# Seven products earlier for one pair, and another cut of the stores of turned pages

## The chip, the cores and the metric

The kernel runs on one core of a Trainium2 chip. The metric is the device time of one execution in microseconds (us); of several runs the median is taken. A profile is one more execution, taken with the hardware profiler.

## What is computed

The reference is a two-layer encoder over 256 tokens with a model width of 4096, all in float32. Cut to what matters:

```python
for l in range(2):
    h = rmsnorm(x, norm_w[l])
    proj = h @ w_in[l]                       # 256 x 4096 @ 4096 x 11264
    aq, ak, av, ag, rq, rk, rv, rg = split(proj)
    # attention: 16 query heads on 4 key heads, norm and rotation of q and k
    a_out = silu(ag) * gqa_attention(rope(rmsnorm(aq)), rope(rmsnorm(ak)), av)
    # retention: 8 heads, forward and backward decays
    r_out = silu(rg) * rmsnorm(bidirectional_retention(rope(rq), rope(rk), rv))
    x = x + concat(a_out, r_out) @ w_out[l]  # 256 x 4096 @ 4096 x 4096
return rmsnorm(x, final_norm)
```

The two projections of each layer hold nearly all of the arithmetic.

## The kernel before

**Blocks, pairs, products.** A projection is cut into blocks of 1024 output columns: 11 for `w_in` and 4 for `w_out` in each layer, 30 blocks that the text numbers 0 to 29 by `plan.index` (layer 0: 0 to 10 and 11 to 14; layer 1: 15 to 25 and 26 to 29), or counts from 0 within its projection. The sum over 4096 runs over 16 pairs of 128-row slices. For one pair, a block is a product of a 2 x 2 by a 2 x 2 arrangement of 128 x 128 and 128 x 512 tiles. Such a product can be made with eight tile products, or with seven by taking sums of tiles first (Strassen and Winograd). Each tile product is three matmuls of 128 x 512, because float32 numbers are split into a high and a low part of a shorter format (hi x hi, lo x hi and hi x lo).

**Weight pages.** A pair of eight reads two pages of weights of 128 x 1024 in a block, named A and B. A pair of seven has four: A, B and the sums T and U. Each page goes through a raw buffer (`wraw`, loaded by DMA from SP's queue; sums in `wsum`, made on VectorE), a cast on ScalarE (`whi`) and a subtraction on VectorE (`wlo`). Some B pages are fetched and split through POOL's queue instead (`fhi`, `flo`).

**Operand forms.** `x` is kept in SBUF in the forms that the products need: `x8h`, `x8l` and a third form `x3` for pairs of eight, `x7h`, `x7l` with seven forms for pairs of seven. Four tables say which pair takes seven:

- `SEVEN`: pairs that take seven everywhere.
- `AFTER`: one dictionary for the input projection and one for the output projection; `{10: (3, 1)}` says that pair 10 takes seven from block 3 on in layer 0 and from block 1 on in layer 1. A pair that starts with eight is converted by `sevenfold` when its last product of the block before has been issued.
- `EXTRA`: pair 4, which is kept in the form of eight and converted with more room.
- `WIDE`: all pairs whose operand has room for seven forms. It is the same set before and after.

`DEFER` puts off the third form (`third`) of the pairs of layer 0 until block 2; blocks 0 and 1 of layer 0 use other eight products that don't need it.

**The order of work.** The order of the instructions on each engine is fixed when the program is built. TensorE's products follow the order of pages of each block (`ORDERS`, or `in_groups` where there is none). All other steps are placed around them by a planner, which keeps a model of the engines and of the DMA queues and picks, whenever VectorE or ScalarE is free in its model, the step with the earliest due time (`pump`). `SETS` changes the planner's settings in single blocks: `SOFT` is the due time of ordinary steps, `PE_REST` how long the inputs of a small attention product should have been ready before TensorE takes it up. Engines wait only on semaphores, each in its own order.

**Turned pages.** Attention and retention work with transposed pages. `turned` transposes blocks of 32 x 32 on VectorE within SBUF; `store` then writes the page (128 x 1024) to DRAM so that the rest of the transposition is done by the addresses, in four DMAs on POOL's queue; `fetch` or a later read brings it back, when all four have landed. The DRAM tiles are `p_dram`, `q_dram`, `g_dram`, `k_dram`, `rk_dram`, `rq_dram` and `next_dram`. Every instruction is recorded by a helper on line 463, so the profile names all of them L463; tiles tell them apart.

Of the kernel before, what the change touches and what calls it, by code (L numbers as in the profile page):

```python
# [19 lines left out]
SEQ = 256  # L20
# [13 lines left out]
BLK = 32  # L34
# [14 lines left out]
SOFT = 7.0  # L49
# [3 lines left out]
PE_REST = 3.0  # L53
# [12 lines left out]

SPLITS = 3

SEVEN = (0, 2, 5, 8, 11, 13)

MORE = ()

AFTER = ({10: (3, 1)}, {4: (1, 1), 10: (1, 1)})

EXTRA = (4,)

WIDE = tuple(sorted({*SEVEN, *MORE, *AFTER[0], *AFTER[1]} - {*EXTRA}))

# [8 lines left out]
FORMS = 2  # L87

ORDERS = {
# [21 lines left out]

SETS = {
    (0, 'PE_REST'): 2.0,
    (1, 'SLACK'): 2.0,
    (5, 'PE_REST'): 4.0,
    (6, 'PE_REST'): 4.0,
    (8, 'DUE'): 50.0,
# [102 lines left out]
def sevens_of(l, second, b):  # L220

    late = [_p for _p, _b in AFTER[second].items() if b >= _b[l]]
    return tuple(sorted({*SEVEN, *(MORE if second else ()), *late}))


def parsed(text):

    return [(int(_v[:-1]), "ATBU".index(_v[-1])) for _v in text.split()]


def in_groups(sevens, first=False):

    order = []
    for group in [tuple(range(_a, _b)) for _a, _b in zip(sevens, sevens[1:] + (NP,))]:
        one, rest = group[:1], group[1:]
        if first:
            order += [(_p, _k) for _p in NATIVE if _p in group for _k in (PAGE_A, PAGE_B)]
            one = [_p for _p in one if _p not in NATIVE]
            rest = [_p for _p in rest if _p not in NATIVE]
        one = [(_p, _k) for _p in one for _k in (PAGE_A, PAGE_T, PAGE_B, PAGE_U)]  # L240
        rest = [(_p, _k) for _p in rest for _k in (PAGE_A, PAGE_B)]
        for _v in one:
            order += [_v] + rest[:1]
            rest = rest[1:]
        order += rest
    return order


def slots_of(order, sevens, first=False, plain=False):

    for _p, _k in order:
        if _p in sevens and not (first and _p in NATIVE):
            yield [(_b, _p, (ALL, _a), _k, _h) for _b, _a, _pg, _h in SEVEN_PRODUCTS if _pg == _k]
        else:
            eight = PLAIN_PRODUCTS if plain else EIGHT_PRODUCTS
            yield [(_b, _p, (_i, _a), _k, _h) for _b, _i, _a, _pg, _h in eight if _pg == _k]
# [273 lines left out]
def hybrid_encoder(  # L530
# [14 lines left out]
    ve, ac, pe, gp, sy = (  # L545
        Engine(e, engine, model, active)
        for e, engine in (("V", nc.vector), ("A", nc.scalar), ("P", nc.tensor), ("G", nc.gpsimd), ("S", nc.sync))
    )
# [39 lines left out]
    def drop(n=1):  # L588

        def dropped():  # L590
            held[0] -= n
            own(-n)

        do(dropped)
# [12 lines left out]
    def plan_of(l, second, b):  # L607
# [11 lines left out]
        plan.sevens = sevens_of(l, second, plan.b)  # L619
        pages = parsed(ORDERS[plan.index]) if plan.index in ORDERS else in_groups(plan.sevens, plan.start)  # L620
        for slot in slots_of(pages, plan.sevens, plan.start, plan.plain):
# [404 lines left out]
    def split_pair(p, v, whole, stage):  # L1026
# [56 lines left out]
        else:  # L1083
            late = AFTER[stage % 2].get(p, (None,) * DEPTH)[stage // 2]
            if p in EIGHTS:
# [59 lines left out]
    def sevenfold(p, phase):  # L1145

        while held[0] + pledged() >= PAGES:
            yield
        hi, lo = operand[p][:2]
        v = page([P, 7, P], "xf")  # L1150
        if p in WIDE:
            ve.tensor_add(v[:, :4, :], f32(hi)[:, :4, :], f32(lo)[:, :4, :])
        else:
            both = [f32(w).rearrange("p k (m t) -> p m k t", m=MT) for w in (hi, lo)]
            ve.tensor_add(v[:, :4, :].rearrange("p (m k) t -> p m k t", m=MT), *both)
        yield from forms(v, v[:, 2, :], v[:, A22N, :])
        if p in WIDE:
            ac.copy(hi[:, 2:7, :], v[:, 2:7, :])
            yield
            ve.tensor_sub(lo[:, 2:7, :], v[:, 2:7, :], f32(hi)[:, 2:7, :])  # L1160
        else:
            room = operand[p][3].rearrange("p a b t -> p (a b) t")
            if phase not in spare:
                spare[phase] = t(sp, [P, 2 * MT, HD], "cs", dt=F32R)
            n = 2 * EXTRA.index(p)
            more = spare[phase][:, n : n + 2, :]
            halves = hi[:, :, P:], lo[:, :, P:]
            ac.copy(halves[0], v[:, 2:4, :])
            ac.copy(room[:, 0:3, :], v[:, 4:7, :])
            yield  # L1170
            ve.tensor_sub(halves[1], v[:, 2:4, :], f32(halves[0]))
            ve.tensor_sub(room[:, 3, :], v[:, 4, :], f32(room[:, 0, :]))
            ve.tensor_sub(more, v[:, 5:7, :], f32(room[:, 1:3, :]))
            pieces = [(hi[:, k, :P], lo[:, k, :P]) for k in range(2)] + [(hi[:, k, P:], lo[:, k, P:]) for k in range(2)]
            pieces += [(room[:, 0, :], room[:, 3, :])] + [(room[:, 1 + k, :], more[:, k, :]) for k in range(2)]
            do(partial(sevenths.__setitem__, p, pieces))
        drop()
        do(partial(changed.__setitem__, p, phase))
        yield
# [269 lines left out]

    def store(room, to):  # L1450

        to = to.rearrange("(b e) (a f) -> a e b f", e=BLK, a=4)
        for a in range(4):
            gp.dma_start(to[a], room[BLK * a : BLK * (a + 1), :].rearrange("e (b f) -> e b f", b=4))
        drop()

    def fetch(src, name):
# [48 lines left out]
    def rotary(v, L, kind, to):  # L1506
# [34 lines left out]
        drop()  # L1541
        yield
        store(v, to)
        return rs if kind == "aq" else None

# [15 lines left out]
    def attention_pair(g, h, kv, qT, rs, done):  # L1561
# [38 lines left out]
        drop()  # L1600
        yield
        store(room, p_dram[2 * (g % 2) + h // 2])
        yield

# [26 lines left out]
    def attention_group(L, g, gacc, qacc):  # L1631
        def gates():
            yield from gate(gacc, L)
            room = page([P, KG * SEQ], "room")
            turned(gacc, room)
            drop()
            yield
            store(room, g_dram[g % 2])

        yield from gates()  # L1640
        while "aq" not in L.tables:
            yield
        rs = yield from rotary(qacc, L, "aq", q_dram[g % 2])
        yield
        L.rs[g] = rs
# [218 lines left out]
    def block(plan, after_pair, combine, then):  # L1864
# [67 lines left out]
        def there(p):  # L1932
            if first_order and p in NATIVE:
                return p in as_it_comes
            if plan.b >= AFTER[second].get(p, (N_IN,) * DEPTH)[plan.layer] > 0 and changed.get(p) != plan.phase:
                return False
# [32 lines left out]
        def ended(n, name, p, k):  # L1969
# [6 lines left out]
            while over and all(not left[q] for q in range(min(over))):  # L1976
                q = min(over)
                over.remove(q)
                after_pair(q)
                if AFTER[second].get(q, (0,) * DEPTH)[plan.layer] == plan.b + 1:  # L1980
                    one = Lane(sevenfold(q, plan.phase))
# [374 lines left out]
```

## Time and profile before

| | |
|---|---|
| time, median of 3 runs | 2580.09 us (2575.61 to 2580.73) |
| the profiled execution's own time | 2579.86 us |
| its span, first to last instruction | 2578.1 us |
| TensorE (PE) busy | 2562.9 us, 11479 matmuls |
| VectorE (DVE) busy | 2365.2 us |
| ScalarE (ACT) busy | 1708.5 us |
| GpSimd (POOL) busy | 455.5 us |
| DMA | 685.95 MB, 266 GB/s on average |
| mean granted TensorE clock | 0.998 |

A row of a group of instructions names line, engine, operation, what it writes and reads, shapes and count, then busy time, mean time of one in ns, and the idle time before them with what ended it. PEld is TensorE's weight load, which overlaps the matmuls. A row of a wait names who waited for whom, the total in us, how often, and the longest. A row of a DMA gives the kilobytes of one and the median time from issue to landing.

### The profile page before, as it was taken

To read this page: it belongs to the slowest core of one execution; us is meant where nothing else is said; L and a number is where in the kernel's file an instruction comes from. 1 tells how busy PE (TensorE), PEld (TensorE's weight loads), DVE (VectorE), ACT (ScalarE), POOL (GpSimd) and SP (SyncE) were. 2 spreads that over 40 slices of the span, in tenths; PEclk is the share of its full clock that TensorE was granted. 3 is DMA by queue.
4 is the path that set the end of the run, shared out by engine and by line. 5 is a ranking of instruction groups with operands and counts; after the bars stand their busy time and mean duration, and the time that the engine had idled before them with its cause. 6 is when DMAs were issued, how large, how long until landed. Compare 5 with 4: busy or idle time off the path is not lost.

```text
span 2578.1 us, 34225 instructions
## 1 busy us (share of the span) xinstructions
PE 2562.9 (99%) x11479; PEld 2118.9 (82%) x11479; DVE 2365.2 (92%) x2882; ACT 1708.5 (66%) x2482; POOL 455.5 (18%) x672
## 2 busy tenths in 40 slices
PE   9999999999999999999999999999999999999998
PEld 6888888887888888888888888888888888888886
DVE  7999998999989899998999999999999799999887
ACT  7766676666655768665786666775676566776665
POOL 0112221211111111111221112212211111111111
PEclk9999999999999999999999999999999999999999
DMA  8988888888678787988998888888887787888986
GB/s 305 325 258 285 281 268 263 282 271 259 209 237 263 233 279 237 293 263 255 328 309 266 264 276 273 291 251 290 272 270 227 238 250 239 267 260 262 269 261 212
DMA packets 197680, 685.95 MB, mean 266 GB/s; under 512 B 24192, under 2 KB 24448, under 8 KB 197504
## 3 DMA queue, kind: packets, MB, share of 16 engines
q1 hardware_dynamic: 126880, 447.80, 48.9%
q0 software_dynamic: 70624, 235.97, 35.9%
q8 instruction: 90, 1.47, 0.2%
q14 instruction: 86, 0.70, 0.1%
HBM read 636.49 MB, written 47.19 MB: 265 GB/s over the span
## 4 chain that ended last, share of the span: by engine, by line
PE 95%; DMA 2%; DVE 1%; issue 1%; ACT 0%; POOL 0%; POOLq 0%; DVEq 0%; ACTq 0%
PE M L463 91%; PE ps L463 4%; DMA wraw<-in_w_in 1%; DVE wlo L463 1%; DMA pT<-p_dram 0%; DMA flo<-in_w_out 0%; DVE wsum L463 0%; DVE cb L463 0%; ACT whi L463 0%; POOL p_dram L463 0%; DVE ca L463 0%; POOL rs L463 0%; DVE pTl L463 0%; ACT full L463 0%; DVE room L463 0%
## 5 line engine op out<-in xcount | busy, mean ns | idle before, releaser
L463 ACT CAST whi<-wraw 128x1024 fp32r<-128x1024 f32 (+1 forms) x816 | 759.4, 935 | 353.5 <-PE M L463 283.3
L463 DVE TENSOR_TENSOR wlo<-wraw,whi 128x1024 fp32r<-128x1024 f32 (+1 forms) x816 | 868.2, 1075 | 54.0 <-ACT whi L463 50.0
L463 ACT CAST whi<-wsum 128x1024 fp32r<-128x1024 f32 x418 | 438.6, 1050 | 290.7 <-DVE wsum L463 140.5
L463 DVE TENSOR_TENSOR wlo<-wsum,whi 128x1024 fp32r<-128x1024 f32 x418 | 509.3, 1219 | 94.0 <-ACT whi L463 64.0
L463 PE MATMUL M<-whi,x7h 128*128 128x512 f32 x1465 | 571.0, 390 | 2.0 <-DVE ca L463 1.3
L463 PE MATMUL M<-whi,x7l 128*128 128x512 f32 x1465 | 570.4, 389 | 0.0
L463 PE MATMUL M<-wlo,x7h 128*128 128x512 f32 x1465 | 476.4, 389 | 0.1
L463 PE MATMUL M<-whi,x8h 128*128 128x512 f32 x1168 | 455.1, 390 | 0.0
L463 PE MATMUL M<-whi,x8l 128*128 128x512 f32 x1168 | 454.8, 389 | 0.2 <-DVE x8l L463 0.2
L463 PE MATMUL M<-wlo,x8h 128*128 128x512 f32 x1168 | 362.2, 389 | 0.0
L463 PEld LDWEIGHTS M<-whi,x7h 128*128 128x128 f32 x1465 | 275.1, 188 | 60.4 <-ACT whi L463 3.0
L463 PEld LDWEIGHTS M<-wlo,x7h 128*128 128x128 f32 x1465 | 274.7, 188 | 58.3 <-DVE wlo L463 1.2
L463 PEld LDWEIGHTS M<-whi,x7l 128*128 128x128 f32 x1465 | 275.1, 188 | 56.3 <-issue 0.2
L463 DVE TENSOR_TENSOR wsum<-wraw 128x1024 f32<-128x1024 f32 x209 | 254.5, 1218 | 4.2 <-DMA wraw<-in_w_out 2.3
L463 PEld LDWEIGHTS M<-whi,x8h 128*128 128x128 f32 x1168 | 219.3, 188 | 46.3 <-DVE ca L463 1.2
L463 PEld LDWEIGHTS M<-wlo,x8h 128*128 128x128 f32 x1168 | 219.2, 188 | 45.7
L463 PEld LDWEIGHTS M<-whi,x8l 128*128 128x128 f32 x1168 | 219.3, 188 | 45.6 <-DVE x8l L463 0.7
L463 PE MATMUL M<-whi,x 128*128 128x512 f32 x742 | 229.6, 389 | 0.0
L463 ACT ACTIVATE flo<-fhi 128x1024 fp32r<-128x1024 f32 (+1 forms) x140 | 147.0, 1050 | 121.4 <-PE M L463 120.5
L463 POOL DMA_DIRECT2D fhi<-in_w_in x102 | 56.6, 554 | 878.2 <-PE M L463 877.6
L463 PEld LDWEIGHTS M<-whi,x 128*128 128x128 f32 x742 | 138.8, 188 | 28.7
L463 PE MATMUL M<-fhi,x8l 128*128 128x512 f32 x414 | 161.1, 389 | 0.0
(275 smaller groups left out, 3179.7 us busy)
## 6 DMA issues: line engine op xcount, KB each, us to landing
wraw<-in_w_in SPq DMA_DIRECT2D x598, 512.0 KB, 5.8
wraw<-in_w_out SPq DMA_DIRECT2D x218, 512.0 KB, 6.0
fhi<-in_w_in POOLq DMA_DIRECT2D x102, 512.0 KB, 4.7
flo<-in_w_in POOLq DMA_DIRECT2D x102, 512.0 KB, 8.2
fhi<-in_w_out POOLq DMA_DIRECT2D x35, 512.0 KB, 5.6
flo<-in_w_out POOLq DMA_DIRECT2D x35, 512.0 KB, 8.0
full<-next_dram POOLq DMA_DIRECT2D x24, 512.0 KB, 8.4
p_dram<-room POOLq DMA_DIRECT2D x64, 128.0 KB, 5.2
```

Source lines behind the costliest of these rows:

```text
L463: op.call()
```

## The change

Three things are changed. Pair 10 takes seven products from block 1 on in layer 0's input projection (before: from block 3 on) and in all four blocks of its output projection (before: from block 1 on). Pair 2 leaves `SEVEN` and is listed in `AFTER` instead: seven everywhere as before, but in layer 0's output projection from block 2 on only. Page orders for blocks 1 and 3 are added, those for 11 and 19 replaced, and two settings are added, for blocks 0 and 2. And `store` cuts a page into four parts of 128 partitions by 256 columns instead of 32 partitions by 1024 columns.

```diff
-SEVEN = (0, 2, 5, 8, 11, 13)
+SEVEN = (0, 5, 8, 11, 13)
...
-AFTER = ({10: (3, 1)}, {4: (1, 1), 10: (1, 1)})
+AFTER = ({2: (0, 0), 10: (1, 1)}, {2: (2, 0), 4: (1, 1), 10: (0, 1)})
...
 ORDERS = {
+    1: '0A 0T 1A 1B 0B 0U 2A 3A 2T 3B 2B 4A 2U 4B 5A 6A 5T 5B 6B 7A 5U 7B 8A 9A 8T 9B 8B 8U 10A 10T 10B 10U 11A 12A 11T 12B 11B 11U 13A 14A 13T 14B 13B 13U 15A 15B',
+    3: '0A 0T 1A 1B 0B 0U 2A 3A 2T 3B 2B 4A 2U 4B 5A 6A 5T 6B 5B 7A 8A 5U 7B 9A 8T 9B 8B 8U 10A 10T 10B 10U 11A 12A 11T 12B 11B 11U 13A 14A 13T 14B 13B 13U 15A 15B',
...
-    11: '0A 0T 0B 1A 1B 0U 2A 3A 2T 3B 2B 4A 2U 4B 5A 6A 5T 6B 5B 7A 5U 7B 8A 9A 8T 9B 8B 10A 8U 10B 11A 12A 11T 12B 11B 11U 13A 14A 13T 14B 13B 13U 15A 15B',
-    19: '0A 0T 1A 1B 0B 0U 2A 3A 2T 3B 2B 4A 2U 4B 5A 6A 5T 6B 5B 7A 5U 7B 8A 9A 8T 9B 8B 8U 10A 12A 10T 10B 10U 11A 11T 12B 11B 11U 13A 14A 13T 14B 13B 13U 15A 15B',
+    11: '0A 0T 1A 1B 0B 2A 0U 2B 3A 3B 4A 4B 5A 6A 5T 6B 5B 7A 5U 7B 8A 9A 8T 10A 9B 8B 8U 10T 10B 10U 11A 12A 11T 12B 11B 11U 13A 14A 13T 14B 13B 13U 15A 15B',
+    19: '0A 0T 1A 1B 0B 0U 2A 3A 2T 3B 2B 4A 2U 4B 5A 6A 5T 6B 5B 7A 5U 7B 8A 9A 8T 9B 8B 8U 10A 12A 10T 10B 11A 11T 12B 10U 11B 11U 13A 14A 13T 14B 13B 13U 15A 15B',
...
 SETS = {
     (0, 'PE_REST'): 2.0,
+    (0, 'SOFT'): 3.0,
     (1, 'SLACK'): 2.0,
+    (2, 'PE_REST'): 4.0,
...
     def store(room, to):
-        to = to.rearrange("(b e) (a f) -> a e b f", e=BLK, a=4)
-        for a in range(4):
-            gp.dma_start(to[a], room[BLK * a : BLK * (a + 1), :].rearrange("e (b f) -> e b f", b=4))
+        to = to.rearrange("(b e) (a f) -> b a e f", e=BLK, a=4)
+        for b in range(4):
+            gp.dma_start(to[b], room[:, b * SEQ : (b + 1) * SEQ])
         drop()
```

## The prediction

> **What bounds the kernel now.** I read the page's busy times and its chain first, then the chain in order of time, then TensorE's waits, then stretches of one block each.
>
> ```profile
> span 2578.1 us, 34225 instructions
> PE 2562.9 (99%) x11479; PEld 2118.9 (82%) x11479; DVE 2365.2 (92%) x2882; ACT 1708.5 (66%) x2482; POOL 455.5 (18%) x672
> ...
> PE 95%; DMA 2%; DVE 1%; issue 1%; ACT 0%; POOL 0%; POOLq 0%; DVEq 0%; ACTq 0%
> ...
> L463 DVE TENSOR_TENSOR wsum<-wraw 128x1024 f32<-128x1024 f32 x209 | 254.5, 1218 | 4.2 <-DMA wraw<-in_w_out 2.3
> ```
>
> TensorE is busy in all but 15.2 us of the span, and it is 95% of the chain that ended last. The last row counts the seven-product pairs: one such sum for each, 209 in all. A busy TensorE can still be slowed, so the chain in order of time gives its pace:
>
> ```profile
> 598.17 9.73 DMA wraw<-in_w_in
> ...
> 722.18 144.41 PE M L463 x637
> ...
> 1046.05 455.59 PE M L463 x2007
> ```
>
> 455.59 us for 2007 matmuls and 144.41 for 637 are both 0.227 us for one 128x512 matmul. The pace is even; only the number of matmuls and the few waits can move the time. TensorE's own waits are short:
>
> ```profile
> PE M L463 <- DVE ca L463: 1.3, 2, 0.8
> PE ps L463 <- DVE junk L463: 1.1, 1, 1.1
> PE M L463 <- DMA flo<-in_w_out: 0.8, 1, 0.8
> PE M L463 <- ACT whi L463: 0.5, 1, 0.5
> PE ps L463 <- DVE pTl L463: 0.4, 1, 0.4
> ```
>
> They come to 4.1 us; no waiting product is named for the rest of the 15.2. VectorE is second. Blocks are recognised by counting matmuls; the stretches below are blocks 1, 2 and 3 of layer 0, and blocks 1 and 2 of its output projection:
>
> ```profile
> 94.50:177.40 82.90, 82.90 (x367) 68.66 (x366) 81.80 (x131) 52.63 (x81) 15.39 (x21) 1.00 0.92 283
> 177.40:263.30 85.90, 85.90 (x391) 71.55 (x390) 80.32 (x104) 58.41 (x95) 18.20 (x27) 1.00 0.85 269
> 263.30:350.00 86.70, 86.70 (x389) 71.84 (x388) 79.04 (x89) 57.38 (x86) 18.56 (x27) 1.00 0.86 267
> ...
> 1044.80:1127.50 82.70, 82.24 (x362) 67.15 (x361) 77.83 (x89) 49.42 (x60) 13.75 (x20) 1.00 0.87 275
> 1127.50:1209.10 81.60, 81.60 (x362) 67.57 (x361) 71.85 (x77) 48.77 (x58) 15.13 (x22) 1.00 0.91 278
> ```
>
> Columns after the stretch: length, then busy time of PE, PEld, DVE, ACT, POOL, then the granted clock. In block 1 of layer 0 VectorE is busy 81.80 of 82.90 us, and yet TensorE loses nothing there. The clock is 1.00 throughout.
>
> **The change part by part.** *Products.* A block has 16 pairs, a pair takes eight products or seven, a product is three matmuls. By the new sets, blocks 1 and 2 of layer 0's input projection have seven pairs of seven instead of six: two products less. In its output projection pair 10 replaces pair 2 in block 0 (six either way), and block 1 has seven instead of eight, since pair 2 joins only at block 2: one product more. Layer 1 keeps its counts. Net one product less, 3 x 0.227 = 0.68 us, all of it on the path: **-0.68 us**.
>
> *Work on VectorE and ScalarE in blocks 1 and 2.* One pair of seven needs four weight pages and two sums instead of two pages. The rows are those of block 1:
>
> ```profile
> L463 DVE TENSOR_TENSOR wlo<-wraw,whi 128x1024 fp32r<-128x1024 f32 x21 | 25.3, 1218 | 0.5 <-ACT whi L463 0.3
> L463 DVE TENSOR_TENSOR wlo<-wsum,whi 128x1024 fp32r<-128x1024 f32 x12 | 14.6, 1217 | 0.2 <-ACT whi L463 0.2
> L463 DVE TENSOR_TENSOR wsum<-wraw 128x1024 f32<-128x1024 f32 x6 | 7.3, 1216 | 0.0
> L463 DVE TENSOR_TENSOR wsum<-wsum,wraw 128x512 f32<-128x512 f32 x6 | 4.1, 681 | 0.0
> L463 DVE TENSOR_TENSOR wsum<-wraw,wsum 128x512 f32<-128x512 f32 x6 | 4.1, 681 | 0.0
> L463 DVE TENSOR_TENSOR wlo<-wraw,whi 128x512 fp32r<-128x512 f32 x6 | 4.1, 677 | 0.0
> ...
> L463 DVE TENSOR_TENSOR x3f<-x3f 128x256 f32<-128x256 f32 x6 | 2.5, 410 | 0.1
> ```
>
> Seven: 1.218 + 0.677 + 2 x 1.217 + 1.216 + 2 x 0.681 = 6.91 us; eight: 2 x 1.218 = 2.44; so **+4.47 us** of VectorE in each of the two blocks. ScalarE gets one and a half more casts of about a microsecond in each, in stretches where it is busy 52.63 and 58.41 us: free. The weights that are loaded stay the same pages, so SP's queue has the same loads.
>
> *The operand of pair 10.* Its conversion from eight to seven (sevenfold) moves from the end of block 2 to the end of block 0, and its third form, which block 2 would have used, falls away:
>
> ```profile
> 164.85 0.42 DVE L463 TENSOR_TENSOR x3f<-x7h 128x256 f32<-128x256 f32 x1
> 165.19 0.42 DVE L463 TENSOR_TENSOR x3f<-x7l 128x256 f32<-128x256 f32 x1
> ...
> 170.26 0.41 DVE L463 TENSOR_TENSOR x7l<-x3f,x7h 128x256 fp32r<-128x256 f32 x1
> ...
> 236.43 0.69 DVE L463 TENSOR_TENSOR xf<-x7h,x7l 128x512 f32<-128x512 f32 x1
> 239.95 0.42 DVE L463 TENSOR_TENSOR xf<-xf 128x256 f32<-128x256 f32 x1
> 242.11 0.26 DVE L463 SCALAR_TENSOR_TENSOR xf<-xf 128x128 f32<-128x128 f32 x1
> 243.70 0.28 DVE L463 TENSOR_TENSOR xf<-xf 128x128 f32<-128x128 f32 x1
> 245.34 0.78 DVE L463 TENSOR_TENSOR x7l<-xf,x7h 128x640 fp32r<-128x640 f32 x1
> ```
>
> The third form is 0.42 + 0.42 + 0.41 + 0.41 = 1.66 us, the conversion 2.43. Block 1 then holds 81.80 + 4.47 + 2.43 - 1.66 = 87.04 us of VectorE work beside 82.22 us of TensorE; block 2 holds 80.32 + 4.47 - 2.43 = 82.36 beside 85.22. Together 169.40 beside 167.44: **VectorE is over by 1.96 us**, and block 3, with 86.70 - 79.04 = 7.66 us free, can take that. What can slide are steps that no product waits for soon (rotation, transposes, gates); weight splits and combines go first by their due times. Bounds: at best 0, since block 1 at 99% of VectorE cost TensorE nothing; at worst 87.04 - 82.22 = 4.8 us, if nothing slides out of block 1. I take **+0.5**, near the row of block 1.
>
> *Pairs 2 and 10 in the output projection* swap places: one is made in its seven-form at the split, the other converted later, the same instructions. Pair 2's conversion runs between its last use in block 1 and its first in block 2, where VectorE has 81.60 - 71.85 = 9.75 us free; block 1 there loses 4.47 + 2.43 us of work beside its 77.83. Nothing on the path.
>
> *Orders and settings* (indices 0, 1, 2, 3, 11, 19) change no count, only who is late. Every wait of layer 0 is drawn again. Best, the waits for `ca` (1.3) go; worst, as many come again. I take **0**, keeping -1.3 and +1.3.
>
> *The stores.* Each turned page still goes out in four DMAs of 128 KB from POOL's queue, 1 KB runs in DRAM; the order of issue does not depend on it. Seven rows of the DMA list, first and last here, make 232 such DMAs:
>
> ```profile
> p_dram<-room POOLq DMA_DIRECT2D x64, 128.0 KB, 5.2
> ...
> k_dram<-ca POOLq DMA_DIRECT2D x8, 128.0 KB, 4.6
> ```
>
> A fetch of a stored page cannot be issued before all four have landed, and POOL's in-order queue waits with it:
>
> ```profile
> POOL pT L463 <- DMA p_dram<-room: 33.0, 6, 6.8
> POOL rkq L463 <- DMA rq_dram<-cb: 22.1, 4, 7.8
> ...
> ACT whi L463 <- PE M L463: 412.6, 421, 4.6
> ...
> ACT pTh L463 <- DMA pT<-p_dram: 4.7, 5, 2.6
> ```
>
> Ten fetches waited for a store. Of that, 4.7 us reached ScalarE and 0.4 us TensorE (the wait for `pTl`). ScalarE waits 412.6 us for TensorE to free weight buffers, so it is usually ahead and catches up. No row has a store in the new shape. Below: the waits it could end are the 0.4 for `pTl` and the 0.8 us `ca` wait that followed the weight load of 9.73 us at 598.17 (landed late beside a store and its fetch): -1.2. Above: see the second rival, up to +15. I take **+0.3**, near the 0.4 that today's lateness costs.
>
> [...]
>
> Sum: -0.68 + 0.5 + 0 + 0.3 = +0.1 on the profiled execution's 2579.86 (span 2578.1 and 1.8 around it), so **2580.0**. That execution lies 0.2 under the median of the runs, 2580.09.
>
> **The rivals.**
> *VectorE becomes the bound in blocks 1 and 2.* For it: 169.40 beside 167.44 us. Against: block 3 has room. If the excess of block 1 falls on TensorE: 2579.9 - 0.7 + 4.8 = 2584; with the backlog carried through block 2 as well, all 7.3 us added in the two blocks, 2586.5. It shows as slower once more than 5.9 of the 7.3 are uncovered.
>
> *The stores get slower: the rival on the other side.* The new part's DRAM pattern begins with 4 column blocks, not with 32 rows. If the transfer is split along that, it runs on 4 of 16 engines with 32 KB each instead of 8 KB. The queue rows give the rate of an engine:
>
> ```profile
> q1 hardware_dynamic: 126880, 447.80, 48.9%
> q0 software_dynamic: 70624, 235.97, 35.9%
> ```
>
> 447.80 MB in 48.9% of 16 x 2578 us are 22 KB/us, 235.97 MB in 35.9% are 16. So 32 KB take 1.5 to 2.0 us, 8 KB 0.4 to 0.5: each part lands 1.1 to 1.5 us later, the last one too. Ten waiting fetches make 11 to 15 us, 13 in the middle, on top of 2579.7 (the sum without stores): if a tenth reaches TensorE, 2581; a third, 2584; all of it, 2593. It decides (over 0.2%) from 5.3 us on, about 40%. Against it: four parts on four different groups of engines load all sixteen alike. [...]
>
> *The waits go.* -0.68, the 1.3 for `ca`, the 0.4 for `pTl` and the 0.5 for `whi`: 2577.0, still inside 0.2%. The lowest run shown, 2575.61, says that some executions lose less than the profiled one.
>
> **How the numbers follow.** About no change 0.60; waits go 0.12; VectorE 0.13; stores 0.15. This measurement tells 0.2%, 5.2 us, from no change. Waits-go is faster by that in a third of its chance (as in the lowest run): 0.05 with a little of the main case. Slower is half of each of the other two and a little more: 0.17. Range: from the lowest run, 2575.5, up to 2587.5, which takes in VectorE's 2586.5 and the stores up to a bit over half their full price.
>
> **What would show it.** Right: `wsum<-wraw` 210 times instead of 209, three matmuls fewer, 0.227 us apart; VectorE at 99% and more in blocks 1 and 2 with no TensorE waits there; packets between 512 B and 2 KB up by 128 for each of the 232 parts, if a packet is one partition's run. Wrong: TensorE waits for `wlo` or `whi` in blocks 1 or 2; last parts landing over a microsecond later with POOL's waits for `p_dram` above 33.0 us; or new waits at block starts for `ca`.

## The result, and the profile after

The changed kernel takes 2621.93 us (median of four runs, 2617.32 to 2624.73), the one before 2579.62 beside it: a ratio of 1.0164, interval 1.0152 to 1.0177. It is 42 us slower, and outside the predicted range. The profiled execution took 2617.32 us; its span is 37.4 us longer than before. In experiment 3 one execution ran at a granted clock of 0.654 and took 3689.59 us; the numbers there are those of the other three. From the profile's page: busy times, chain, the group of sums, packets, queues and stores.

```profile
span 2615.5 us, 34225 instructions
PE 2575.0 (98%) x11476; PEld 2119.6 (81%) x11476; DVE 2366.0 (90%) x2883; ACT 1703.1 (65%) x2482; POOL 485.1 (19%) x672
...
DMA packets 219954, 686.31 MB, mean 262 GB/s; under 512 B 46465, under 2 KB 46721, under 8 KB 219777
q1 hardware_dynamic: 126880, 447.80, 47.1%
q0 software_dynamic: 92896, 236.33, 37.0%
...
PE 79%; DMA 10%; DVE 4%; issue 4%; ACT 2%; POOL 1%; DVEq 0%; POOLq 0%; SPq 0%; ACTq 0%
...
L467 DVE TENSOR_TENSOR wsum<-wraw 128x1024 f32<-128x1024 f32 x210 | 255.8, 1218 | 27.4 <-DMA wraw<-in_w_in 15.3
...
p_dram<-room POOLq DMA_DIRECT2D x64, 128.0 KB, 8.0
```

TensorE does three matmuls fewer, as forecast, and the sums number 210. But DMA's share of the chain went from 2% to 10%, the parts of `p_dram` land after 8.0 us instead of 5.2, and POOL's queue (q0) has 22272 packets more. TensorE is idle for 40.5 us instead of 15.2 (25.3 more) and "busy" for 12.1 us more although it has less to do. What it waits for, then what VectorE, ScalarE and POOL wait for:

```profile
PE M L467 <- DMA flo<-in_w_in: 6.6, 4, 3.2
PE ps L467 <- DVE pTl L467: 6.1, 7, 2.1
PE M L467 <- DVE ca L467: 4.3, 2, 2.8
PE M L467 <- DMA flo<-in_w_out: 3.1, 3, 2.1
PE ps L467 <- ACT pTh L467: 2.4, 2, 1.8
```

```profile
DVE wsum L467 <- DMA wraw<-in_w_in: 15.3, 14, 3.3
...
ACT pTh L467 <- DMA pT<-p_dram: 27.4, 12, 6.3
...
POOL pT L467 <- DMA p_dram<-room: 48.9, 10, 11.1
```

Two kinds of lateness stand side by side. Stored pages come back late (POOL waits 48.9 us for `p_dram` instead of 33.0, `pT` reaches ScalarE late). And plain weight loads, which read no stored page, are late too (`flo`, `wraw`): TensorE waited for no `flo<-in_w_in` before, and VectorE's row for `wraw` was this:

```profile
DVE wsum L463 <- DMA wraw<-in_w_in: 0.9, 2, 0.5
```

A stretch of the chain in order of time shows the second kind, start, length and what:

```profile
694.75 1.05 POOL next_dram L467 x2
...
696.20 0.69 POOL next_dram L467
...
697.47 0.71 POOL next_dram L467
...
698.83 12.07 DMA flo<-in_w_in
```

Four parts of a store are issued, and the weight load issued right behind them takes 12.07 us; TensorE's next products wait for it. Others took 13.62, 13.88, 15.21 and 15.25 us. The landing times of all `flo` loads, of the kernel before and then of this one, have the same median and another end:

```profile
DMA to landing us min/median/max: 3.9/8.1/11.7
```

```profile
DMA to landing us min/median/max: 3.6/8.1/15.3
```

### The profile page after: what moved, and what is told of

Same layout as the page of the kernel before. It is cut to its first block, busy times and chain, and to the rows that moved or that the text cites. A ratio compares the mean times of both kernels' runs of the same rounds, so it can differ in the third digit from the quotient of the medians.

```text
span 2615.5 us, 34225 instructions
## 1 busy us (share of the span) xinstructions
PE 2575.0 (98%) x11476; PEld 2119.6 (81%) x11476; DVE 2366.0 (90%) x2883; ACT 1703.1 (65%) x2482; POOL 485.1 (19%) x672
## 4 chain that ended last, share of the span: by engine, by line
PE 79%; DMA 10%; DVE 4%; issue 4%; ACT 2%; POOL 1%; DVEq 0%; POOLq 0%; SPq 0%; ACTq 0%
PE M L467 75%; PE ps L467 3%; DMA flo<-in_w_in 2%; DVE wlo L467 2%; DMA p_dram<-room 2%; DMA wraw<-in_w_in 2%; DMA flo<-in_w_out 1%; DMA pT<-p_dram 1%; ACT whi L467 1%; DVE wsum L467 1%; DVE cb L467 0%; DMA next_dram<-room 0%; DMA q_dram<-cb 0%; DVE pTl L467 0%; DMA q<-q_dram 0%
## 5 line engine op out<-in xcount | busy, mean ns | idle before, releaser
L467 DVE TENSOR_TENSOR wsum<-wraw 128x1024 f32<-128x1024 f32 x210 | 255.8, 1218 | 27.4 <-DMA wraw<-in_w_in 15.3
L467 PE MATMUL M<-fhi,x8h 128*128 128x512 f32 x414 | 161.2, 389 | 0.0
```

The costliest lines, as they stand in the source:

```text
L467: op.call()
```

## Experiments

**1. The two halves of the change apart.** The new store in the kernel before, with every instruction in its old order, and the moved pairs with the old store.

```diff
-        to = to.rearrange("(b e) (a f) -> a e b f", e=BLK, a=4)
-        for a in range(4):
-            gp.dma_start(to[a], room[BLK * a : BLK * (a + 1), :].rearrange("e (b f) -> e b f", b=4))
+        to = to.rearrange("(b e) (a f) -> b a e f", e=BLK, a=4)
+        for b in range(4):
+            gp.dma_start(to[b], room[:, b * SEQ : (b + 1) * SEQ])
```

The new store alone:

> The kernel before with the new store alone (same order of instructions on every engine). Theory A (the stores run on 4 of 16 engines): nearly the whole loss, 2615 to 2625 us, POOL's waits for p_dram and TensorE's waits for pTl and flo as in the changed kernel, last parts landing 8 to 15 us after the first issue. Rival (the move of pair 10 overloads VectorE in blocks 1 to 3 of layer 0): 2580 to 2590, with the waits in blocks 3 to 7 gone.

The moved pairs alone:

> The changed kernel with the old store: the pair tables, orders and settings alone. Theory A: 2576 to 2582 us, one product less (0.7 us) and other small waits; VectorE at 99% in blocks 1 and 2 of layer 0 without TensorE waits. Rival (VectorE): 2584 or more, with TensorE waits for wlo or ca in blocks 1 to 3.

The store alone took 2617.93 us against 2578.95, ratio 1.0149 (1.0134 to 1.0163): 39.0 of the 42.3 us, and the intervals of the two ratios overlap. The pairs alone took 2578.33, ratio 0.9997 (0.9988 to 1.0006). The pairs alone in blocks 1 and 2 (length, then PE, PEld, DVE, ACT, POOL, clock), and their TensorE waits:

```profile
94.40:177.30 82.90, 82.60 (x364) 68.05 (x363) 82.31 (x123) 53.39 (x80) 14.70 (x20) 1.00 0.92 279
177.30:262.00 84.70, 84.70 (x383) 70.23 (x382) 83.09 (x108) 57.58 (x89) 17.10 (x25) 1.00 0.83 254
```

```profile
PE M L467 <- DMA fhi<-in_w_in: 1.2, 1, 1.2
PE M L467 <- DVE ca L467: 1.1, 2, 0.7
```

VectorE is busy 99% of block 1 and 98% of block 2, and TensorE idles 0.3 us there. With the store alone, TensorE waits most for weight loads:

```profile
PE M L463 <- DMA flo<-in_w_in: 14.0, 7, 2.9
PE ps L463 <- DVE pTl L463: 4.2, 4, 2.3
```

**2. What in the store costs: the cut or the pattern.** The new store differs from the old in two things. The source is cut by columns, 128 partitions by 256, instead of 32 partitions by 1024; and the DRAM pattern begins with 4 instead of 32. Four kernels vary one each; each moves the same bytes and leaves out the rearrangement that the later steps need.

```diff
 # 128 partitions by 256, pattern begins with 128
+            gp.dma_start(to[:, b * SEQ : (b + 1) * SEQ], room[:, b * SEQ : (b + 1) * SEQ])
 # 32 partitions by 1024, pattern begins with 4, a block of columns
+        to = to.rearrange("(d c) (a f) -> a c d f", c=4, a=4)
 # 128 partitions by 256, pattern begins with 4, a block of columns of all rows
+        to = to.rearrange("(d c) (b f) -> b c d f", c=4, b=4)
 # 32 partitions by 1024, pattern begins with 4, 32 whole rows
+        to = to.rearrange("(b e) (a f) -> b a e f", e=BLK, a=4)
```

The wide cut, beginning with 128:

> The kernel before, its pages cut into 128 partitions by 256 columns as in the changed kernel, but each part written to 128 rows of DRAM, a row of 1 KB for each partition, so that both patterns begin with 128 (the rearrangement of the page is left out, so the fetched pages hold other values). Theory A: all 16 engines, 2575 to 2582 us, no packets of 16 bytes. Rival B (short runs from 128 partitions are slow in themselves): as slow as the changed kernel, 2610 to 2625.

The old cut, beginning with 4:

> The kernel before with its old cut of 32 partitions by 1024 columns, but the DRAM pattern of each part begins with a count of 4 (4 x 32 rows of 1 KB; the rows are permuted, so the fetched pages hold other values). Theory A: slow like the changed kernel, 2610 to 2625 us, with 96 packets of 16 bytes for each part. Rival B: as the kernel before, 2575 to 2582.

The wide cut, beginning with 4, other DRAM addresses:

> The kernel before with pages cut into 128 partitions by 256 columns as in the changed kernel, the DRAM pattern beginning with 4 as there, but the 1 KB pieces of a part going to one column block of all 128 rows (as with the old cut) instead of to 32 whole rows; rows permuted, so the fetched pages hold other values. Theory A1 (four engines that each read 32 partitions in 1 KB runs are what costs): as slow as the new store alone, 2612 to 2622 us. Theory A2 (four engines that write side by side into the same 4 KB rows of DRAM are what costs): as the old cut on four engines, 2583 to 2592.

The old cut, beginning with 4, whole rows:

> The fourth of the set: the old cut of 32 partitions by 1024 columns, written on four engines to 32 whole rows of DRAM, as the changed kernel's parts are (values in other places, so the fetched pages hold other values). Theory A1 (reading 32 partitions an engine costs): 2583 to 2592 us. Theory A2 (DRAM side): 2612 to 2622. Theory A3 (only the lateness of the last part counts, from whatever cause): the time goes with the median of the last part's landing, 2588 at 10.4 us and 2618 at 11.3.

| cut | begins with | DRAM side | time | ratio |
|---|---|---|---|---|
| 128 x 256 | 128 | columns | 2578.00 | 0.9994 (0.9985 to 1.0003) |
| 32 x 1024 | 4 | columns | 2587.95 | 1.0039 (1.0027 to 1.0050) |
| 32 x 1024 | 4 | rows | 2586.53 | 1.0029 (1.0017 to 1.0041) |
| 128 x 256 | 4 | columns | 2614.85 | 1.0134 (1.0116 to 1.0152) |
| 128 x 256 | 4 | rows (the change) | 2617.93 | 1.0149 (1.0134 to 1.0163) |

The wide cut itself is free on this evidence, and which addresses a part fills makes no difference that can be told. A pattern that begins with 4 costs 7 to 9 us with the old cut, far less than I had expected, and 35 to 39 with the wide one. Packets of the kernel that begins with 128, then of the old cut beginning with 4, with the landing times of the `p_dram` parts of each:

```profile
DMA packets 197681, 685.96 MB, mean 266 GB/s; under 512 B 24192, under 2 KB 24448, under 8 KB 197504
...
L463 POOL DMA_DIRECT2D p_dram<-room x64: 539/542/927, 246.0 to 1835.2; - x64
DMA to landing us min/median/max: 2.0/5.5/12.0
```

```profile
DMA packets 219952, 686.30 MB, mean 265 GB/s; under 512 B 46464, under 2 KB 46720, under 8 KB 219776
...
L463 POOL DMA_DIRECT2D p_dram<-room x64: 735/882/1455, 247.5 to 1842.6; - x64
DMA to landing us min/median/max: 3.6/6.8/12.8
```

All four kernels of the table that begin with 4 have 46464 small packets; the one that begins with 128 has the 24192 of the kernel before. The difference, 22272, is 96 for each of the 232 parts, and they are of 16 bytes. A part still has its 32 packets of 4 KB; if 4 of the 16 engines carry them, that is 8 for each, and 96 is 8 for each of the other 12. So the small packets fit engines that carry no data; the traces do not name a packet's engine, and the engine counts given below are this reading of the packets. POOL's time to issue one part (here 542 and 882 ns in the middle, 682 in the changed store alone) does not go with the loss: the longest belongs to the cheaper kernel.

**3. The dose.** The same stores with patterns that begin with 8 (wide cut) and with 2 (old cut): by that reading 8 engines and 2.

```diff
 # 128 partitions by 256
+        to = to.rearrange("(d c) (b f) -> b c d f", c=8, b=4)
 # 32 partitions by 1024
+        to = to.rearrange("(d c) (a f) -> a c d f", c=2, a=4)
```

Begins with 8:

> The kernel before with parts of 128 partitions by 256 columns, whose DRAM pattern begins with 8 instead of 4 (rows permuted, the fetched pages hold other values). Theory A (the first count sets the number of engines): 8 engines with 16 KB each, 64 packets of 16 bytes for each part instead of 96, last part landing at 8.5 to 10 us, 2580 to 2592 us. If it were the cut of 128 partitions whenever fewer than 16 engines work: as with 4, 2610 to 2620.

Begins with 2:

> The kernel before with its old cut of 32 partitions, the DRAM pattern beginning with 2 (values in other places). Theory A: two engines with 64 KB each, 112 packets of 16 bytes for each part. If the time goes with how late the last part lands: at 13 to 17 us, 2630 to 2680. If only the cut of 128 partitions makes it dear: below 2600.

Eight: 2581.85 us, ratio 1.0010 (1.0001 to 1.0019), 2.9 us. Two: 2780.45, ratio 1.0787 (1.0769 to 1.0805), 201 us, far above what I had expected. The wide cut, then, costs 2.9 us on 8 engines and 35 to 39 on 4, the old one 7 to 9 on 4 and 201 on 2. Packets of the one and of the other, and what TensorE did with two, then what POOL waited for with two:

```profile
DMA packets 205105, 686.07 MB, mean 266 GB/s; under 512 B 31616, under 2 KB 31872, under 8 KB 204928
```

```profile
DMA packets 249648, 686.78 MB, mean 247 GB/s; under 512 B 76160, under 2 KB 76416, under 8 KB 249472
...
PE 2626.0 (94%) x11479; PEld 2150.6 (77%) x11479; DVE 2369.6 (85%) x2882; ACT 1704.0 (61%) x2482; POOL 570.0 (20%) x672
...
PE M L463 <- DMA flo<-in_w_in: 59.3, 14, 10.9
PE M L463 <- ACT whi L463: 22.4, 8, 11.8
```

```profile
POOL next_dram L463 <- issue: 94.9, 21, 8.5
POOL p_dram L463 <- issue: 75.2, 23, 7.1
```

Beyond the 24192 of the kernel before, the small packets are 7424 = 232 x 8 x 4 and 51968 = 232 x 14 x 16: as many for an idle engine as a working one has packets of data, (16 - k) x 32/k for k engines. My expected counts for these two were worked out with a wrong rule; this one fits all three.

With two engines something new comes in. POOL stops before parts of a store, for up to 9.4 us, without a wait that the profile names ("issue"): 302 us over all stores, against 0.2 with four engines and the same cut. `flo` loads land after at most 13.9 us there, less than the 15.3 of the changed kernel, and yet TensorE waits 59.3 us for them; so they were issued late. The 201 us are therefore no third point on one curve, and what stops POOL is not shown.

**4. Which stores.** The new store for `p_dram` alone, and for `next_dram` alone, 16 of the 58 stored pages each.

```diff
+        if any(to is v for v in p_dram):
+            to = to.rearrange("(b e) (a f) -> b a e f", e=BLK, a=4)
+            for b in range(4):
+                gp.dma_start(to[b], room[:, b * SEQ : (b + 1) * SEQ])
+        else:
...
```

`p_dram`:

> The kernel before with the new store for p_dram alone, 16 of the 58 stores, whose pages are fetched at once. If late landings of pages that are fetched at once cost: more than their share of 39 us (11), 15 to 30, so 2594 to 2609 us. If contention of the stores with the weight loads costs: about 11 us, 2590.

`next_dram`:

> The kernel before with the new store for next_dram alone, 16 of the 58 stores, of which one had its fetch waiting in the kernel before (1.5 us). If late landings cost: 2579 to 2583 us. If contention with the weight loads costs: about 11 us, 2590.

They took 11.2 us (2590.75, ratio 1.0043, 1.0026 to 1.0059) and 7.5 us (2587.05, ratio 1.0029, 1.0018 to 1.0040). Sixteen fifty-eighths of 39 us are 10.8. The 7.5 lie between the two forecasts, 0 to 3 for late pages and 11 for held-up loads. The loss is spread over the stores, roughly by their number, and is not tied to the pages that attention waits for.

**5. Late pages, or late everything?** If the loss is that stored pages come back late, an order of work that reckons with it should win some of it back. The planner's model of a store's landing gets 3.6 us added; once with the new store, once with the old.

```diff
+STORE_LATE = 3.6
...
+        one.end = t + RING_AFTER[ring] + LATER + one.late
```

New store:

> The kernel before with the new store, and a planner that reckons with 3.6 us more until a store has landed (the difference of the medians of the last part's landing, 11.3 and 7.7). If the loss is that of steps placed too early for pages that come later than planned: most of it goes, 2583 to 2598 us. If it is the weight loads that are held up beside a store (7.8 instead of 6.5 us): little changes, 2608 to 2622.

Old store:

> The control for it: the old store with the planner that reckons with 3.6 us more. The price of waiting longer in the plan alone: 2576 to 2586 us in both theories.

2619.79 (ratio 1.0157, 1.0142 to 1.0172) and 2582.90 (1.0018, 1.0008 to 1.0027). Between them lie 36.9 us, about the 39 of experiment 1. The plan did its part, for POOL's waits for `p_dram` are 33.7 us instead of the 87.7 of the store alone. But planning for late pages recovers no time that can be told.

Then the other way round: the real stores keep the old form, and each page is also copied, from the same buffer, to a DRAM tile that nobody reads; that copy in the old form (16 engines), in the new one (4 engines), and on 4 engines with the old cut (27904 packets under 512 B with the first, 50176 with each of the others, again 22272 more).

```diff
+        more = idle_dram.rearrange("(b e) (a f) -> b a e f", e=BLK, a=4)
+        for b in range(4):
+            gp.dma_start(more[b], room[:, b * SEQ : (b + 1) * SEQ])
```

On 16:

> The kernel before, whose stores go out in the old form and are then written a second time, in the old form too, to a DRAM page that nobody reads. It is the base for the next two, which differ from it in the form of the second, idle copy alone. Both theories: 2580 to 2610 us (30 MB more to write, and a page is released later).

On 4, as in the change:

> The same with the idle copy in the new form (128 partitions, four engines). Nobody waits for it except the release of its page; the page that is fetched goes out on 16 engines. Theory C (the new store costs by what it holds up on its four engines: weight loads and POOL's later transfers): 25 to 40 us over the run with the idle copy on 16. Theory L (it costs because a stored page is there later): within 6 us of it.

On 4, the old cut:

> The same with the idle copy on four engines, but cut into 32 partitions by 1024 columns. Theory C: 5 to 12 us over the run with the idle copy on 16, as the store of that form itself; theory L: within 6 us of it.

2591.80 (ratio 1.0052, 1.0035 to 1.0069), 2623.20 (1.0175, 1.0156 to 1.0194) and 2609.41 (1.0116, 1.0097 to 1.0135). An idle copy costs 12.2 us by itself; on 4 engines 31.4 us more, with the old cut 17.6 more, which is above what I had expected. The real stores' last parts landed after 7.88 us (median) with the copy on 16 engines and 8.24 with it on 4. The loads of weights beside them, first with 16, then with 4:

```profile
wraw<-in_w_in SPq DMA_DIRECT2D x598, 512.0 KB, 6.0
...
idle_dram<-room POOLq DMA_DIRECT2D x160, 128.0 KB, 7.3
```

```profile
wraw<-in_w_in SPq DMA_DIRECT2D x598, 512.0 KB, 6.6
...
idle_dram<-room POOLq DMA_DIRECT2D x160, 128.0 KB, 9.3
```

So 31 of the 39 us come back though no page that is read is stored in the new way. Pages do reach TensorE late (it waits 8.1 us for `pTl` instead of 2.2), but their fetches are loads beside the copies and take longer themselves (`pT` 8.5 us instead of 7.2). Two things beside it moved too. The page's buffer comes free later, but VectorE has no wait for an idle copy in these traces. And POOL waits longer for the copies (24.7 us instead of 17.5); with the old cut it waits as long (25.5), though that run is 13.8 us faster. That makes neither likely as the main cause, but this experiment does not shut them out.

**Where the loads are held up.** From the landing times of all loads, those that overlap a store in flight by more than a microsecond and the rest, mean us; after it the median landing of a store's last part, counted from the issue of its first:

| store | `wraw` beside | `wraw` else | `flo` beside | last part | loss |
|---|---|---|---|---|---|
| before | 6.49 | 5.83 | 8.20 | 7.72 | |
| the moved pairs alone | 6.79 | 5.84 | 8.42 | 7.74 | -0.6 |
| 8 engines, wide cut | 6.87 | 5.86 | 8.94 | 8.95 | 2.9 |
| 4 engines, old cut, columns | 6.99 | 5.87 | 9.25 | 10.42 | 9.0 |
| 4 engines, wide cut (store alone) | 7.79 | 5.89 | 10.33 | 11.33 | 39.0 |
| the changed kernel | 7.90 | 5.90 | 10.17 | 11.27 | 42.3 |
| 2 engines, old cut | 7.00 | 5.78 | 10.34 | 15.91 | 201 |

Loads away from stores are as fast as ever (`wraw` 5.78 to 5.90 us in every row). Beside a store on four engines, `wraw` loses half a microsecond with the old cut and 1.3 to 1.4 with the wide one, and between these two the loss goes with it. The mean alone does not set the loss: the moved pairs alone stand at 6.79 and lose nothing, and with two engines it is 7.00 beside a loss of 201 us. `flo` loads are issued on POOL's queue behind the parts, so their lateness could also be that of the queue; `wraw` comes by SP's queue and is late as well. The kernel before has no packet of 16 bytes (its 24192 small ones have 4), so by the count of experiment 3 its loads would run on all 16 engines. Each load has 16 landing updates in the trace, the last of which is taken as its landing. Beside a store the first one of `wraw` comes after 5.18 us in the changed kernel instead of 4.72, the last after 7.90 instead of 6.49 (means). That the last ones belong to the four engines that also carry a part's 32 KB each is my estimate from the counts and these times, and not shown: the traces here were not split by engine. Why the wide cut hurts more on the same number of engines stays open.

## Why the prediction was wrong

- *Products, -0.68 us:* right. 11476 matmuls and 210 sums, and the pairs alone lie 0.62 us below the kernel before, which is inside the noise.
- *VectorE in blocks 1 and 2, +0.5:* right within its bounds. TensorE idles 0.3 us in the two blocks of the pairs alone, where it idled for none before. VectorE was busy there for 165.40 us and not for the 169.40 of the sum; block 3 after them has 81.89 instead of 79.04. Its rival is out: 99% and 98% busy, 0.3 us lost.
- *Swap of pairs 2 and 10, orders and settings, 0:* right in sum. Of the waits for `ca` 1.1 us stayed, and one for `fhi` of 1.2 came.
- *The stores, +0.3:* **the step that failed.** It measured +39. The step took a value "near the 0.4 that today's lateness costs", far down in -1.2 to +15, and dropped the four engines, which the packet counts fit, for an argument, "four parts on four different groups of engines load all sixteen alike". Over a whole store that may even out the bytes; the loads in flight beside it still landed 1.3 us later in the mean. Which engines each part took, the traces do not show.
- *The slower-stores rival* had the split that the packet counts fit: four working engines where the pattern begins with 4 (22272 packets of 16 bytes), as eight and two where it begins with 8 and 2 (7424 and 51968), and all 16 where both patterns begin with 32 or 128 (none). But its price was wrong: its upper end was 2593, for it counted only the ten fetches that wait for a stored page. In experiment 5 most of the loss came back with the real stores in their old form, so their own lateness is the smaller part. What the price left out is every other transfer in flight beside a store.
- *Landing:* forecast 1.1 to 1.5 us later for each part, the last one too. The first part of a store lands after 5.41 us instead of 3.95 (median), as forecast; the last lands 3.6 us later, counted from the issue of the first. Why the later parts lose more is not shown.
- *Signs:* the sign for "wrong" was right (POOL's waits for `p_dram` 48.9, above 33.0). The sign of VectorE at 99% and more held in block 1 and fell short in block 2 (98%). The packet sign failed: none appeared between 512 B and 2 KB. Packets of data stayed at 4 KB and the new ones have 16 bytes.

No version here beats both kernels: the moved pairs with the old store are equal to the kernel before.

## What to carry to other kernels

Look at the first counts of both patterns before reshaping a store, even if every run of bytes stays the same. For the stores on POOL's queue here, first counts of 32 and 128 came without packets of 16 bytes, and 128 cost nothing that can be told (ratio 0.9994); a first count of 8 cost 2.9 us, one of 4 cost 7 to 39, one of 2 cost 201. Price such a store not by who waits for it but by everything that is in flight beside it: here 31 of 39 us came back with copies that nobody reads. A counterargument that only balances totals ("the four groups even out") is no ground to take a cost at its low end.

## What the runs showed of the hardware that was not expected

**TensorE's clock was halved after short waits.** Part of the loss is neither a wait nor work. Two stretches of the changed kernel (length, PE, PEld, DVE, ACT, POOL, granted clock), then the chain at the second:

```profile
311.00:314.60 3.60, 1.08 (x4) 0.34 (x4) 1.41 (x2) 2.49 (x3) 0.00 (x0) 1.00 1.04 308
314.60:318.00 3.40, 3.40 (x9) 2.62 (x10) 3.37 (x5) 0.65 (x2) 0.00 (x0) 0.50 0.41 154
...
1615.00:1618.50 3.50, 0.94 (x5) 0.43 (x3) 2.29 (x2) 0.00 (x0) 0.53 (x1) 1.00 1.03 390
1618.50:1625.30 6.80, 6.17 (x15) 4.88 (x16) 0.69 (x1) 3.11 (x4) 0.88 (x1) 0.50 0.47 133
```

```profile
1603.87 15.21 DMA flo<-in_w_in
...
1619.13 5.92 PE M L467 x13
```

Before the second a weight load of 15.21 us starves TensorE, before the first the fetch of a stored page does (8.11 us, behind a `p_dram` part of 16.03), and then the clock is 0.50 for 6.8 and 3.4 us: 13 matmuls take 5.92 us, 0.455 each instead of 0.227. All such stretches of the traces, the fall at the very end of each aside, lie on a fixed grid of 3.413 us. The clock fell after a window with at most 6 matmuls begun in it (15 fill one) and at most 1.74 us busy; in these traces it never fell after a busier one, and it stayed up after some with as little as 1.50 us busy. There are 47 such falls, in eight traces. Some of the kernels:

| kernel | us at half clock | matmuls begun in it | TensorE idle |
|---|---|---|---|
| before, pairs alone, 128 x 256 beginning with 128 | 0 | 0 | 14 to 16 |
| the changed kernel | 10.2 | 23 | 40.5 |
| store alone | 13.7 | 32 | 39.5 |
| begins with 2 | 160.4 | 244 | 159.0 |

At 0.227 us extra for each matmul that makes, as an estimate, 5.2 us in the changed kernel, 7.3 with the store alone and 55 with two engines, which is about half of what experiment 3 lies above its forecast. Of the changed kernel's 37.4 us, then, 25.3 are idle time and about 5.2 the clock, and three matmuls fewer take 0.7 off. The other 7.6 us fit wait that is recorded as busy time: a matmul of 128x512 is recorded with a mean of 0.39 us, though at the even pace the next one starts after 0.227, so the beginning of each wait counts as work. From start to start, away from the half clock, 111 intervals between matmuls are over 0.3 us instead of 58, and they hold 32.6 us more beyond the pace, about the idle time and those 7.6 us together.
